# A hybrid attention layer on one core: loads of the opening in other pieces and places, columns of the modulation moved between projections, and gated linear attention's decay scans spread over its levels

## The chip, the cores and the metric

The kernel runs on one core of a Trainium2 chip. The metric is device time in microseconds for one execution. TensorE (PE) multiplies, VectorE (DVE) and ScalarE (ACT) do the elementwise work, GpSimd (POOL) does a little of it and issues some loads, and SyncE (SP) issues nearly all loads.

## The reference

One layer of a diffusion transformer in fp32, with 256 latent tokens and 256 context tokens of width 2048:

```python
h  = rms_norm(x,   g_mix) * (1 + scale_x) + shift_x      # scale, shift from silu(c) @ w_mod
hc = rms_norm(ctx, g_mix) * (1 + scale_c) + shift_c
qa, ka, va, qb, kb, vb, rb, lrf, lrb, gate_a, gate_b = split(h @ w_in)   # and of hc
o_attn = windowed_attention(qa, ka, va, cka, cva, sink)  # 16 heads, 4 for keys, sink logit
gf = log_sigmoid(lrf @ w_gate_f + b_gate_f) / 16         # 4 heads of 256; gb for the other way
o_gla = gla(qb, kb, vb, gf, gb)                          # both directions, from context's end states
x = x + gate * merge(o_attn, o_gla, rb, gate_a, gate_b)  # w_attn_o, w_gla_o, w_out
x = x + gate2 * conv_ffn(modulate(x, ...))               # w_up, conv of width 3, SwiGLU, w_down
```

Gated linear attention (GLA) weighs the product of a query and a key by the exponential of the decay summed between their two tokens.

## The kernel before, in words

**Weights.** A block of `w_in` of 256 rows by 512 columns is loaded as fp32 (`raw`, `wload`), split by ACT into a rounded part `whi` and by DVE into the rest `wlo` (`wsplit_raw`), and multiplied in three products: high by high, high by low of the tokens, low by high (`proj_nat`, `proj_T`). All loads of a queue go out in program order. The engines' orders are set when the kernel is built: mostly by a scheduler that follows the program, and in places by hand (`in_order`, `pin`).

**The opening.** 1 MB loads of `w_mod` (`mraw`) give the columns of scale and shift: `mod_both` makes one step per load. A step's products (`pm`) go into one bank; behind the last step DVE transposes it (`mtr`), and `end` turns it back to columns on PE (`pcol`). Groups of 2, 2, 4, 4 and 4 tiles of 128 channels follow each other: for each, the scale's columns, then the shift's, then `affine_scale` and `affine_shift` (tokens `xr` into `h00hi`, `h00lo` for the latent ones, `h10hi`, `h10lo` for context), then the group's part of four projections: GLA's queries (QB), keys (KB) and values (VB) of its first half. In the first group, a0, a1, ea are the two steps and the end of the scale, b0, b1, eb those of the shift. Sums of squares for the norm are products `pr`. `idle(n)` puts n products without use (`warm`) onto PE. In later groups the steps of the next group's columns stand in the middle of the projections: `mid` takes the next number from a list,

```python
steps = iter([1, 2, 1, 2, 2, 0])
```

and does so many steps of `bg_steps`.

**GLA.** Behind the groups, four projections go on, each beside one GLA head (`with_gla`). The head is a generator, `gla_A`: it goes on by one `yield` at a fraction of the projection's ticks, 0.91. First come the gates (`pz`, with a chain on ACT and DVE), then eight levels: at level `lv` DVE and ACT make queries and keys that carry the decay inside segments of 2^lv tokens (`q2`, `k2`, segment sums `segs`), and one level later PE multiplies them (`pa`), from which DVE takes a mask's part (`at`). At the end come the context's keys: two running sums of the decay (`kf`, `kg`, scans on DVE), exponentials on ACT, multiplications by the keys, and PE's last `pa`. Between ticks a second list of steps works at the rate `bg_rate`: columns of later modulations on DVE (`mod_latent`, the row at L365) with loads of their own.

**POOL's queue.** The attention sink is loaded by POOL's first DMA, rows of 16 numbers to each partition. Other small loads (`cw`, `lm`, the gates' weights) stand behind `gate`, an instruction on POOL that waits for the last columns.

Of the kernel before, what the change touches and what calls it, by code (L numbers as in the profile page):

```python
# [31 lines left out]
def layer_kernel(ctx, tc, A, out):  # L32
# [90 lines left out]
    def load_tokens(s):  # L123
        for i in range(4):
            k = slice((i % 2) * 4, (i % 2) * 4 + 4)
            load(xr[2 * s + i // 2][:, k, :], A["ctxT" if s else "xT"][i // 2, :, k, :])

# [61 lines left out]
    def wload(src):  # L189
        n = src.shape[0] // P  # L190
        raw = wr.tile([P, 2, 512], F32, name="raw", tag="raw")
        load(raw[:, 0:n, :], src.rearrange("(c p) d -> p c d", p=P))
        return raw

# [110 lines left out]


    def mod_both(part, t0, n, dst, put=None):

        a = []
        w = n * P  # L310
        nk = 16 // n

        def step(k0):
            if k0 == 0:
                a.append(bank(f"pm{part}_{t0}", (P, w), side=True))
            raw = M("mraw", [P, nk, w])
            load(raw, A["w_mod01"][part, t0 + k0 // nk].rearrange("p (c d) -> p c d", c=nk))
            for k in range(nk):
                kt = k0 + k
                q = 32 * (kt % 4)  # L320
                mm_b(a[0][q:q + 32, :], cS[:, kt, :], raw[:, k, :], start=(kt < 4), stop=(kt >= 12))
            if k0 == KT - nk:
                tr = W2("fb", "mtr", [P, n, 4, 32])
                V.transpose(tr.rearrange("p a b c -> p (a b c)"), a[0])
# [71 lines left out]
    def rms_scale(ss, n, shape):  # L396
# [15 lines left out]
    mods = [[mod_both(part, t0, n, dst, put) for part, dst in ((1, scale1), (0, shift1))]  # L412
            for (t0, n), put in zip(groups, [None, None] + 3 * [lambda fn: defer(0, fn)])]

# [4 lines left out]
    def square_sums(s):  # L419
# [3 lines left out]
        for i in range(4):  # L423
            x_ = xr[2 * s + i // 2][:, (i % 2) * 4:(i % 2) * 4 + 4, :]
            q = wr.tile([P, 4, T], F32, name="sq", tag="raw")
            if s + i:
                S.activation(q, x_, AF.Square)
# [55 lines left out]
    def affine_scale(s, t0, n):  # L483
        sc = scale1[:, s, t0:t0 + n]
        V.scalar_tensor_tensor(sc, sc, 1.0, gm1[:, t0:t0 + n], op0=ALU.add, op1=ALU.mult)
        for kt in range(t0, t0 + n):
            xk = xr[2 * s + kt // 8][:, kt % 8, :]
            V.scalar_tensor_tensor(xk, xk, scale1[:, s, kt:kt + 1], rrow1[s], op0=ALU.mult, op1=ALU.mult)

# [39 lines left out]
    factor_row(pr)  # L529
    a0()  # L530
    a1()
    idle(4)
    ea()
    b0()
    affine_scale(0, *groups[0])
    b1()
    raws = [wload(w_in[0:2 * P, c:c + 512]) for c in (QB, QB + 512)]
    idle(4)
# [5 lines left out]
    early.extend(raws)  # L544
    raws = [wload(w_in[0:2 * P, c:c + 512]) for c in (KB, VB)]
    load_tokens(1)
    i, j = affine_shift(0, *groups[0])
    hold.append(i)
    hold_hi.extend([None, j])
    proj_T(w_in, QB, kts, [h_all(0)], add_to(lambda i: qb0[i], True))  # L550
    proj_T(w_in, QB + 512, kts, [h_all(0)], add_to(lambda i: qb0[2 + i], True))
    wk, wv = wsplit_raw(raws[0]), wsplit_raw(raws[1])
# [43 lines left out]
    for gi, (t0, n) in enumerate(groups):  # L596
# [8 lines left out]
        if gi + 1 < len(groups):  # L605
# [3 lines left out]
            if gi == 1:  # L609
                bg_rate[:] = [0.0, 0.0]  # L610
                steps = iter([1, 2, 1, 2, 2, 0])

                def mid():
                    pin[0] = last[0]
                    for _ in range(next(steps)):
                        bg_steps.pop(0)()
                    pin[0] = None
        if t0 == 8:
            more_h(1)
        for s in range(2):  # L620
            if gi > 1:
                affine_scale(s, t0, n)
                affine_shift(s, t0, n)
            if s == 0:
# [80 lines left out]
    def gla_A(h, kb, qb, res):  # L705
# [7 lines left out]
        for d in range(2):  # L713
            g_ = W2("fc", "gc", [P, 2, T])
            for dt in range(2):
# [10 lines left out]
                V.tensor_tensor((PF if d == 0 else SB)[:, dt, :], mn[:, 0:T], e[:, 0:T], op=ALU.add)  # L726
# [30 lines left out]
        for lv in range(8):  # L757
# [21 lines left out]
            V.tensor_tensor(pfR, pfR, pfL[:, :, m - 1:m].to_broadcast([P, n, m]), op=ALU.add)  # L779
            V.tensor_tensor(sbL, sbL, sbR[:, :, 0:1].to_broadcast([P, n, m]), op=ALU.add)  # L780
# [14 lines left out]
        kf = W2("fa", "kf", [P, 2, T])  # L795
        kg = W2("fa", "kg", [P, 2, T])
        tot = sm.tile([P, 2], F32, name="tot", tag="tot", bufs=2)
        one = ones[:, 0:1].to_broadcast([P, T])
        for dt in range(2):
            V.tensor_tensor_scan(kf[:, dt, :], one, gc[0][:, dt, :], 0.0, op0=ALU.mult, op1=ALU.add)  # L800
            V.memset(kg[:, dt, 0:1], 0.0)
            V.tensor_tensor_scan(kg[:, dt, 1:T], ones[:, 0:1].to_broadcast([P, T - 1]), gc[1][:, dt, 0:T - 1], 0.0,
                                 op0=ALU.mult, op1=ALU.add)
        V.tensor_scalar(tot, kf[:, :, T - 1], -1.0 / 16, None, op0=ALU.mult)
        for dt in range(2):
            S.activation(kf[:, dt, :], kf[:, dt, :], AF.Exp, scale=1.0 / 16, bias=tot[:, dt:dt + 1])
        S.activation(kg, kg, AF.Exp, scale=-1.0 / 16)
        V.tensor_tensor(kf, kf, kc, op=ALU.mult)
        V.tensor_tensor(kg, kg, kc, op=ALU.mult)
        yield  # L810
# [39 lines left out]
    bg_steps.extend(mod_latent(((3, shift2), (4, scale2), (2, gcol1))))  # L850
    bg_rate[:] = [0.3, 0.0]

# [39 lines left out]
    G.dma_start(norms[:, 1, :], A["k_norm"][0].partition_broadcast(P))  # L892
    sink = cst.tile([P, 16], F32, name="sink")
    G.dma_start(sink, A["attn_sink"][0].partition_broadcast(P))
    for i, r in enumerate((rq, rk)):
# [131 lines left out]

    bg_rate[0] = 0.52
    rg = rms_scale(ssg, 512, [P, 4, 2])
# [288 lines left out]
```

## Time and profile before

| | us |
|---|---|
| time, median of 3 runs | 1982.68 (1981.75 to 1982.88) |
| the profiled execution | 1981.3 |
| its span | 1979.5 |
| PE busy | 1955.1 |
| DVE busy | 1399.8 |
| ACT busy | 972.1 |
| POOL busy | 44.2 |

The stages in the span: 0 to 25 us tokens' norm and the first columns; 25 to 73 the first group's projections, context's norm and the next columns; 73 to 204 the other groups; 204 to 460 GLA's four heads beside projections; then attention, the output projections and the ConvFFN, up to 1979.5. Rows of the stages give the busy time of each engine, with the number of instructions, then the clock that PE was granted (1.00 is full), the share of the DMA engines and GB/s. Rows of waits give the engine and the tile that waited, for which engine and tile it waited, the total, the number and the longest. In rows of the timeline a bracket holds the idle time before and what ended it. Durations overlap where instructions are pipelined.

### The profile page before, as it was taken

The page shows a single profiled execution, that of the slowest core. Times are in us where ns is not written, and L with a number is a line of the kernel's source. Part 1 is how long each engine was busy: PE and PEld are TensorE (multiplying, and loading weights), DVE is VectorE, ACT ScalarE, POOL GpSimd, SP SyncE. Part 2 cuts the span into 40 slices and gives each one's busy share as a digit, 9 for nine tenths or more (in the row PEclk, how much of TensorE's full clock was granted, in tenths as well). Part 3 has the DMA queues.
Part 4 walks back from the last instruction along what each step waited for, and adds up shares of the span by engine and source line. Part 5 has one row for each costly group of instructions (what it writes and reads, how often), then busy time and mean ns, then how long its engine had stood idle before and what let it go on. Part 6 is the DMA issues. An engine that isn't in the chain of part 4 may idle for free.

```text
span 1979.5 us, 27075 instructions
## 1 busy us (share of the span) xinstructions
PE 1955.1 (99%) x10292; PEld 1636.0 (83%) x10292; DVE 1399.8 (71%) x2150; ACT 972.1 (49%) x1415; POOL 44.2 (2%) x60
## 2 busy tenths in 40 slices
PE   7999999999999999999999999999999999999999
PEld 5679988888887778888888888888888888888887
DVE  5756767876767988777766467989886555677754
ACT  4323555552345666444444445755555334555533
POOL 0010010012000000000000000000000000000000
PEclk9999999999999999999999999999999999999999
DMA  9966222336754456888888677688886566666563
GB/s 379 413 258 185 75 85 78 93 108 205 233 160 118 127 181 213 268 290 292 289 286 265 235 236 262 198 271 285 257 274 228 193 197 188 187 190 189 188 216 109
DMA packets 183666, 420.88 MB, mean 213 GB/s; under 512 B 12544, under 2 KB 12768, under 8 KB 178800
## 3 DMA queue, kind: packets, MB, share of 16 engines
q1 hardware_dynamic: 182000, 413.45, 63.9%
q0 software_dynamic: 1360, 5.54, 1.0%
q8 instruction: 80, 1.31, 0.3%
q14 instruction: 50, 0.41, 0.1%
q10 hardware_dynamic: 176, 0.17, 0.0%
HBM read 416.98 MB, written 2.13 MB: 212 GB/s over the span
## 4 chain that ended last, share of the span: by engine, by line
PE 68%; DVE 0%; ACT 0%; issue 0%; DVEq 0%
PE acc L83 52%; PE accs L83 12%; PE poa L95 1%; PE pS L95 1%; PE ptp L98 1%; PE pto L98 0%; PE ptx L98 0%; DVE wlo L208 0%; ACT s L986 0%; PE ptq L98 0%; DVE s L991 0%; DVE yd L1238 0%; DVE yd L1232 0%; DVE raw L365 0%; ACT whi L207 0%
## 5 line engine op out<-in xcount | busy, mean ns | idle before, releaser
L208 DVE TENSOR_TENSOR wlo<-raw,whi 128x1024 fp32r<-128x1024 f32 x568 | 694.1, 1223 | 439.9 <-ACT whi L207 396.4
L207 ACT ACTIVATE whi<-raw 128x1024 fp32r<-128x1024 f32 x568 | 601.5, 1060 | 765.9 <-PE acc L83 608.9
L83 PE MATMUL accs<-h,whi 128*128 128x512 f32 x704 | 176.3, 392 | 0.0
L83 PE MATMUL acc<-h,whi 128*128 128x512 f32 x640 | 160.4, 392 | 0.0
L83 PEld LDWEIGHTS accs<-h,whi 128*128 128x128 f32 x704 | 126.6, 189 | 22.7
L83 PE MATMUL acc<-whi,h01hi 128*128 128x512 f32 x352 | 139.9, 398 | 0.0
L83 PE MATMUL acc<-whi,h00hi 128*128 128x512 f32 x352 | 138.9, 395 | 0.0
L83 PE MATMUL acc<-whi,h00lo 128*128 128x512 f32 x352 | 138.1, 392 | 0.0
L83 PE MATMUL acc<-whi,h01lo 128*128 128x512 f32 x352 | 137.8, 392 | 0.0
L83 PE MATMUL acc<-whi,ah 128*128 128x512 f32 x352 | 137.0, 389 | 0.0
L83 PE MATMUL acc<-whi,al 128*128 128x512 f32 x352 | 137.0, 389 | 0.0
L83 PEld LDWEIGHTS acc<-h,whi 128*128 128x128 f32 x640 | 115.0, 189 | 20.6
L83 PEld LDWEIGHTS accs<-h,wlo 128*128 128x128 f32 x704 | 96.0, 190 | 6.9
L83 PE MATMUL acc<-wlo,h01hi 128*128 128x512 f32 x352 | 98.7, 396 | 0.0
L83 PE MATMUL accs<-h,wlo 128*128 128x256 f32 x704 | 98.2, 282 | 0.0
L83 PE MATMUL acc<-wlo,h00hi 128*128 128x512 f32 x352 | 97.8, 394 | 0.0
L83 PE MATMUL acc<-wlo,ah 128*128 128x512 f32 x352 | 94.3, 389 | 0.0
L83 PEld LDWEIGHTS acc<-h,wlo 128*128 128x128 f32 x640 | 87.4, 190 | 6.3
L83 PE MATMUL acc<-h,wlo 128*128 128x256 f32 x640 | 89.4, 282 | 0.0
L365 DVE CUSTOM_DVE_ANT_0 raw<-raw,csrow,pack 128x1024 f32<-128x1024 f32 x64 | 81.4, 1281 | 0.0
L83 PEld LDWEIGHTS acc<-whi,ah 128*128 128x128 f32 x352 | 66.1, 188 | 13.7
L83 PEld LDWEIGHTS acc<-whi,al 128*128 128x128 f32 x352 | 66.1, 188 | 13.7
(377 smaller groups left out, 3558.1 us busy)
## 6 DMA issues: line engine op xcount, KB each, us to landing
raw<-in_w_in SPq DMA_DIRECT2D x208, 512.0 KB, 4.2
raw<-in_w_up SPq DMA_DIRECT2D x176, 512.0 KB, 4.1
raw<-in_w_modT SPq DMA_DIRECT2D x128, 512.0 KB, 4.4
raw<-in_w_down SPq DMA_DIRECT2D x88, 512.0 KB, 3.6
mraw<-in_w_mod SPq DMA_DIRECT2D x32, 1024.0 KB, 12.1
raw<-in_w_attn_o SPq DMA_DIRECT2D x32, 512.0 KB, 5.0
raw<-in_w_gla_o SPq DMA_DIRECT2D x32, 512.0 KB, 5.1
raw<-in_w_out SPq DMA_DIRECT2D x32, 512.0 KB, 4.7
```

The lines of the kernel that those rows point to most:

```text
L83: r = pe_seq(PE.matmul(*a, **k))
L95: return pe_seq(after(PE.matmul(*a, **k)))
L98: return pe_seq(after(PE.transpose(*a)))
L207: j = S.activation(hi[:, 0:n, :], raw[:, 0:n, :], AF.Copy).ins
L208: i = V.tensor_tensor(lo[:, 0:n, :], raw[:, 0:n, :], hi[:, 0:n, :].bitcast(F32), op=ALU.subtract).ins
L365: i0 = V.tensor_tensor_reduce(out=raws[i], in0=raws[i], in1=row[0], scale=1.0, scalar=d if h else bmod[:, b0:b0 + 1], op0=ALU.mult, op1=AL ...
```

## The change

Loads of the opening:

```diff
-        for i in range(4):
-            k = slice((i % 2) * 4, (i % 2) * 4 + 4)
-            load(xr[2 * s + i // 2][:, k, :], A["ctxT" if s else "xT"][i // 2, :, k, :])
+        for i in range(2):
+            load(xr[2 * s + i], A["ctxT" if s else "xT"][i])
...
+    def first_w(i):
+        raw = wr.tile([P, 2, 512], F32, name="raw", tag="raw")
+        load(raw.rearrange("p k d -> p (k d)"), A["w_first"][i])
+        return raw
...
+            if t0 < 4 and part == 0 and k0:
+                load(raw[:, 0:nk // 2, :], src[:, 0:nk // 2, :])
+                load(raw[:, nk // 2:nk, :], src[:, nk // 2:nk, :])
+            else:
+                load(raw, src)
...
+    data["w_first"] = np.stack([data["w_in"][0, 0:2 * P, c:c + 512].reshape(2, P, 512).transpose(1, 0, 2).reshape(P, 1024)
+                                for c in (QB, QB + 512, KB, VB)])
```

Tokens are loaded in two pieces of 1 MB, and a partition's row is 8 KB instead of 4; the first four blocks of `w_in` lie in memory so that a row is 4 KB instead of 2; the second load of the shift of the first two groups is cut in two.

Order of the opening: `idle(6)` is put in twice, squares of the context are ordered behind the evacuation of the first queries, the second group's columns and the context's keys change places:

```diff
     a0()
+    idle(6)
     a1()
     idle(4)
     ea()
     b0()
     affine_scale(0, *groups[0])
+    idle(6)
     b1()
...
-    a0()
     add_up(0, 2)
     factor_row(pr)
+    a0()
     a1()
     affine_scale(1, *groups[0])
     affine_shift(1, *groups[0])
+    b0()
     ea()
-    b0()
-    b1()
-    for s in range(2):
-        affine_scale(s, *groups[1])
+    affine_scale(0, *groups[1])
     early.extend([wk, wv])
-    proj_T(w_in, KB, kts, [h_all(1)], lambda i, b: S.activation(half(i, T), pair_of(b), AF.Copy), mid=eb)
+    proj_T(w_in, KB, kts, [h_all(1)], lambda i, b: S.activation(half(i, T), pair_of(b), AF.Copy), mid=b1)
+    eb()
...
+    affine_scale(1, *groups[1])
...
-                steps = iter([1, 2, 1, 2, 2, 0])
+                steps = iter([1, 2, 1, 4, 0, 0])
+                also = iter([next_columns] * 3 + [scale_2, next_columns, lambda: affine_shift(0, *groups[2])])
```

`next_columns` does a pending `end` of the third group; `scale_2` does that and the third group's `affine_scale`.

On PE, around the context's keys (`acc<-h10hi`), the second group's columns (`pm_2`, `pcol_2`) stood like this before:

```order
L95 MATMUL pm_2_389<-mraw,cS 32x256 x8
L448 MATMUL pr<-sq,ones 128x256 x2
L95 MATMUL pm_2_389<-mraw,cS 32x256 x8
L95 MATMUL pcol_2_429<-mtr,pack 32x16
L95 MATMUL pm_2_436<-mraw,cS 32x256 x16
L83 MATMUL acc<-h10hi,whi 128x256
```

and now stand like this (with the rest of the keys' products between the last `acc` that is shown first and the next `pm`):

```order
L462 MATMUL pr<-sq,ones 128x256 x2
L95 MATMUL pm_2_408<-mraw,cS 32x256 x16
L95 MATMUL pm_2_438<-mraw,cS 32x256 x8
L95 MATMUL pcol_2_449<-mtr,pack 32x16
L83 MATMUL acc<-h10hi,whi 128x256
...
L95 MATMUL pm_2_438<-mraw,cS 32x256 x8
L83 MATMUL acc<-h10hi,wlo 128x256 x8
L95 MATMUL pcol_2_500<-mtr,pack 32x16
```

The norm's sums came to the front, and the last eight column products went from before the keys into their middle.

On PE, in the second group's keys (`acc<-h10lo,whi` is the last product with the high part), the third group's shift (`pm_4`) before:

```order
L83 MATMUL acc<-h10lo,whi 128x256
L95 MATMUL pm_4_673<-mraw,cS 32x512 x8
L83 MATMUL acc<-h00hi,wlo 128x256
...
L95 MATMUL pm_4_673<-mraw,cS 32x512 x8
L95 MATMUL pcol_4_724<-mtr,pack 32x32
L83 MATMUL acc<-whi,h00hi 128x512
```

and now:

```order
L83 MATMUL acc<-h10lo,whi 128x256
L95 MATMUL pcol_4_676<-mtr,pack 32x32
L95 MATMUL pm_4_693<-mraw,cS 32x512 x16
L83 MATMUL acc<-h00hi,wlo 128x256
...
L95 MATMUL pcol_4_740<-mtr,pack 32x32
L83 MATMUL acc<-whi,h00hi 128x512
```

All 16 products of the shift stand in one place now, ahead of the 16 products with the low part, and the products with `whi` on the left that follow are the values.

The sink's load moves behind the gate, and in GLA the gates are made in four pieces instead of two, the scans and keys are made inside the levels, and the rates change:

```diff
+    sink = cst.tile([P, 16], F32, name="sink")
+    G.dma_start(sink, A["attn_sink"][0].partition_broadcast(P))
     lmask = cst.tile([P, 7, P], U8, name="lmask")
...
+                yield
             gc.append(g_)
-            yield
+
+        kf = W2("fb", "kf", [P, 2, T])
+        kg = W2("fb", "kg", [P, 2, T])
...
+        beside_levels = [[], [lambda i: scan_f(0, i)], [lambda i: scan_f(1, i)],
+                         [lambda i: scan_g(0, i), decay_f], [lambda i: scan_g(1, i)], [keys_f], [keys_g], []]
...
-            if lv == 1:
-                yield
             if lv:
                 products(lv - 1, *prev)
             prev = q2, k2
+            for fn in beside_levels[lv]:
+                fn(level)
             yield
...
-    bg_rate[:] = [0.3, 0.0]
+    bg_rate[:] = [0.0, 0.0]
...
-        beside[:] = [gla_A(h, kb, qbt, res), 0.91, 0.0]
+        beside[:] = [gla_A(h, kb, qbt, res), 0.97, 0.0]
...
-    bg_rate[0] = 0.52
+    bg_rate[0] = 0.62
```

`scan_f` and `scan_g` are the scans for one half of the channels, `decay_f` their total and the exponentials, `keys_f` and `keys_g` the multiplications (in `keys_g` behind its exponential), each ordered on DVE behind the last segment sum of its level. During GLA no modulation steps run any more; they run in the output projections at the higher rate.

On DVE, in the third level of the second head, before (`q_2902` and `k_2906` are the level's queries and keys):

```order
L751 COPY_PREDICATED at<-lmask,pa 128x256
L777 TENSOR_TENSOR segs<-segs 128x64x4
L768 TENSOR_TENSOR q_2902<-q_2902,qb 128x512
L775 TENSOR_TENSOR k_2906<-k_2906,kb_109 128x512
L778 TENSOR_TENSOR segs<-segs 128x64x4
L779 TENSOR_TENSOR segs<-segs 128x64x4
```

and now:

```order
L814 COPY_PREDICATED at<-lmask,pa 128x256
L770 SCALAR_TENSOR_TENSOR kf<-ones,gc 128x256
L840 TENSOR_TENSOR segs<-segs 128x64x4
L831 TENSOR_TENSOR q_2932<-q_2932,qb 128x512
L838 TENSOR_TENSOR k_2936<-k_2936,kb_107 128x512
L841 TENSOR_TENSOR segs<-segs 128x64x4
```

A scan (`kf<-ones,gc`) stands between two levels, ahead of the segment sums and the queries.

More of the change, by code (lines that the diff above doesn't have):

```diff
@@ L304, in layer_kernel @@
     ALL = list(range(KT))
+    folded = []
     def mod_both(part, t0, n, dst, put=None):
@@ L316, in step @@
             raw = M("mraw", [P, nk, w])
-            load(raw, A["w_mod01"][part, t0 + k0 // nk].rearrange("p (c d) -> p c d", c=nk))
+            src = A["w_mod01"][part, t0 + k0 // nk].rearrange("p (c d) -> p c d", c=nk)
+            if t0 < 4 and part == 0 and k0:
[3 more added lines that the diff above has]
+                load(raw, src)
             for k in range(nk):
@@ L323, in step @@
                 tr = W2("fb", "mtr", [P, n, 4, 32])
-                V.transpose(tr.rearrange("p a b c -> p (a b c)"), a[0])
+                folded[:] = [V.transpose(tr.rearrange("p a b c -> p (a b c)"), a[0]).ins]
                 a.append(tr)
@@ L412, in layer_kernel @@
     mods = [[mod_both(part, t0, n, dst, put) for part, dst in ((1, scale1), (0, shift1))]
-            for (t0, n), put in zip(groups, [None, None] + 3 * [lambda fn: defer(0, fn)])]
+            for (t0, n), put in zip(groups, [None, None] + [lambda fn: pend.append(fn)] + 2 * [lambda fn: defer(0, fn)])]
+    pend = []
     rrow1 = []
@@ L426, in square_sums @@
             if s + i:
-                S.activation(q, x_, AF.Square)
+                j = S.activation(q, x_, AF.Square).ins
+                if s and i in (0, 2):
+                    in_order(evicted[i + 1], j)
             else:
@@ L487, in affine_scale @@
             xk = xr[2 * s + kt // 8][:, kt % 8, :]
-            V.scalar_tensor_tensor(xk, xk, scale1[:, s, kt:kt + 1], rrow1[s], op0=ALU.mult, op1=ALU.mult)
+            i = V.scalar_tensor_tensor(xk, xk, scale1[:, s, kt:kt + 1], rrow1[s], op0=ALU.mult, op1=ALU.mult).ins
+            if s == 1 and kt < 2:
+                in_order(folded[0], i)
     def affine_shift(s, t0, n):
@@ L535, in layer_kernel @@
     affine_scale(0, *groups[0])
+    idle(6)
     b1()
-    raws = [wload(w_in[0:2 * P, c:c + 512]) for c in (QB, QB + 512)]
+    raws = [first_w(i) for i in range(2)]
     idle(4)
@@ L544, in layer_kernel @@
     early.extend(raws)
-    raws = [wload(w_in[0:2 * P, c:c + 512]) for c in (KB, VB)]
+    raws = [first_w(i) for i in range(2, 4)]
     load_tokens(1)
@@ L549, in layer_kernel @@
     hold_hi.extend([None, j])
-    proj_T(w_in, QB, kts, [h_all(0)], add_to(lambda i: qb0[i], True))
-    proj_T(w_in, QB + 512, kts, [h_all(0)], add_to(lambda i: qb0[2 + i], True))
+    evicted = []
+    for j in range(2):
+        proj_T(w_in, QB + j * 512, kts, [h_all(0)],
+               lambda i, b, j=j: evicted.append(S.activation(qb0[2 * j + i], b, AF.Copy).ins))
     wk, wv = wsplit_raw(raws[0]), wsplit_raw(raws[1])
@@ L610, in layer_kernel, with next_columns, scale_2 @@
                 bg_rate[:] = [0.0, 0.0]
-                steps = iter([1, 2, 1, 2, 2, 0])
+                steps = iter([1, 2, 1, 4, 0, 0])
+                def next_columns():
+                    if pend:
+                        pend.pop(0)()
+                def scale_2():
+                    next_columns()
+                    for s in range(2):
+                        affine_scale(s, *groups[2])
+                also = iter([next_columns] * 3 + [scale_2, next_columns, lambda: affine_shift(0, *groups[2])])
                 def mid():
                     pin[0] = last[0]
+                    next(also)()
                     for _ in range(next(steps)):
@@ L620, in layer_kernel @@
         for s in range(2):
-            if gi > 1:
+            if gi > 2:
                 affine_scale(s, t0, n)
+            if gi > 2 or (gi == 2 and s):
                 affine_shift(s, t0, n)
@@ L727, in gla_A, with scan_f, scan_g, decay_f @@
                 G.tensor_tensor(g_[:, dt, :], mn[:, T:2 * T], e[:, T:2 * T], op=ALU.add)
+                yield
             gc.append(g_)
-            yield
+        kf = W2("fb", "kf", [P, 2, T])
+        kg = W2("fb", "kg", [P, 2, T])
+        def scan_f(dt, level):
+            in_order(level, V.tensor_tensor_scan(kf[:, dt, :], ones[:, 0:1].to_broadcast([P, T]), gc[0][:, dt, :],
+                                                 0.0, op0=ALU.mult, op1=ALU.add).ins)
+        def scan_g(dt, level):
+            V.memset(kg[:, dt, 0:1], 0.0)
+            in_order(level, V.tensor_tensor_scan(kg[:, dt, 1:T], ones[:, 0:1].to_broadcast([P, T - 1]),
+                                                 gc[1][:, dt, 0:T - 1], 0.0, op0=ALU.mult, op1=ALU.add).ins)
+        def decay_f(level):
+            tot = sm.tile([P, 2], F32, name="tot", tag="tot", bufs=2)
+            in_order(level, V.tensor_scalar(tot, kf[:, :, T - 1], -1.0 / 16, None, op0=ALU.mult).ins)
+            for dt in range(2):
+                S.activation(kf[:, dt, :], kf[:, dt, :], AF.Exp, scale=1.0 / 16, bias=tot[:, dt:dt + 1])
+        def keys_f(level):
+            in_order(level, V.tensor_tensor(kf, kf, kc, op=ALU.mult).ins)
+        def keys_g(level):
+            S.activation(kg, kg, AF.Exp, scale=-1.0 / 16)
+            in_order(level, V.tensor_tensor(kg, kg, kc, op=ALU.mult).ins)
+        beside_levels = [[], [lambda i: scan_f(0, i)], [lambda i: scan_f(1, i)],
+                         [lambda i: scan_g(0, i), decay_f], [lambda i: scan_g(1, i)], [keys_f], [keys_g], []]
         at = sm.tile([P, 2, P], F32, name="at", tag="at", bufs=1)
@@ L779, in gla_A @@
             V.tensor_tensor(pfR, pfR, pfL[:, :, m - 1:m].to_broadcast([P, n, m]), op=ALU.add)
-            V.tensor_tensor(sbL, sbL, sbR[:, :, 0:1].to_broadcast([P, n, m]), op=ALU.add)
-            if lv == 1:
-                yield
+            level = V.tensor_tensor(sbL, sbL, sbR[:, :, 0:1].to_broadcast([P, n, m]), op=ALU.add).ins
             if lv:
@@ L794, in gla_A @@
             V.tensor_tensor(dst, dst, q_, op=ALU.mult)
[L795 to L809, printed above, removed]
         yield
@@ L892, in layer_kernel @@
     G.dma_start(norms[:, 1, :], A["k_norm"][0].partition_broadcast(P))
-    sink = cst.tile([P, 16], F32, name="sink")
-    G.dma_start(sink, A["attn_sink"][0].partition_broadcast(P))
     for i, r in enumerate((rq, rk)):
```

## The prediction

> **What bounds the kernel now.** I read the page's first and fourth parts, then the stages, then PE's waits inside the stages that the change touches, and last the timeline around those waits.
>
> ```profile
> span 1979.5 us, 27075 instructions
> PE 1955.1 (99%) x10292; PEld 1636.0 (83%) x10292; DVE 1399.8 (71%) x2150; ACT 972.1 (49%) x1415; POOL 44.2 (2%) x60
> PE 68%; DVE 0%; ACT 0%; issue 0%; DVEq 0%
> ```
>
> PE is the bound: it is busy for 99% of the span, and the chain that ended last lies on it. The change removes no product, so it can gain only what PE stands still or runs slowly. Per stage (microseconds, busy time of PE, PEld, DVE, ACT, POOL, then granted clock, DMA share, GB/s):
>
> ```profile
> 0.00:25.00 25.00, 16.43 (x114) 10.60 (x114) 9.74 (x29) 8.56 (x12) 1.39 (x6) 0.93 0.94 348
> 25.00:44.00 19.00, 17.33 (x154) 13.60 (x154) 13.39 (x24) 12.42 (x19) 0.00 (x0) 1.00 1.02 410
> 44.00:73.00 29.00, 26.83 (x200) 18.87 (x200) 20.90 (x49) 7.93 (x14) 0.00 (x0) 1.00 1.02 416
> 73.00:160.00 87.00, 86.33 (x638) 67.08 (x639) 54.87 (x108) 25.13 (x34) 6.27 (x12) 1.00 0.84 308
> 204.00:460.00 256.00, 250.36 (x1452) 215.42 (x1445) 192.20 (x361) 145.15 (x291) 27.17 (x27) 1.00 0.31 93
> ```
>
> PE is idle for 8.6, 1.7, 2.2, 0.7 and 5.6 us in these rows. Two places are open. Up to 73 us the DMA share is at its full 1.02, so there the loads are the second bound; from 204 to 460 (the four GLA heads beside the projections) DMA is at 0.31 and something else holds PE. PE's waits, first for 0 to 160 us, then for 200 to 460 us (total, times, longest):
>
> ```profile
> PE pm L95 <- DMA mraw<-in_w_mod: 3.0, 3, 1.4
> PE pcol L95 <- DVE mtr L324: 2.6, 4, 0.8
> PE acc L83 <- ACT h10hi L495: 0.7, 1, 0.7
> PE acc L83 <- ACT h00hi L495: 0.4, 1, 0.4
> ```
> ```profile
> PE pa L95 <- DVE q L768: 3.1, 4, 1.1
> PE pa L95 <- DVE kf L808: 2.5, 3, 1.0
> ```
>
> In GLA, 3.1 + 2.5 = 5.6 us, all of PE's idle time there: one wait per head for the first level's queries, and one for the final keys.
>
> **The opening.** The first term is the loads. Throughput between 3 and 11 us (40 slices of 0.2 us), and the share of POOL's queue:
>
> ```profile
> GB/s 365 356 336 404 390 423 348 469 489 348 369 440 177 18 20 20 41 82 205 205 246 451 389 348 389 430 369 369 389 430 328 471 389 492 410 451 410 451 410 420
> q0 software_dynamic: 36, 0.01, 16.6%
> ```
>
> From 5.4 to 7.2 us throughput falls as low as 18 GB/s while 0.01 MB of POOL's small packets (mainly the attention sink) use 16.6% of 16 engines for 8 us: 1.33 us of all engines. Moved behind the gate, the sink lands in the 73 to 160 stage, where DMA is at 0.84, and its first reader comes in attention, far behind: I cost it there at nothing. If that cover failed, it would cost the same 1.33 us.
>
> The second term is bigger rows for tokens and for the first four weight blocks. The nearest rows are the 44 to 73 stage above (416 GB/s, mostly 1 MB loads) and this one, which holds 512 KB loads and 1 MB loads:
>
> ```profile
> 20.00:40.00 20.00, 18.77 (x138) 14.62 (x142) 11.46 (x20) 12.84 (x18) 0.00 (x0) 0.91 1.03 410
> ```
>
> The tokens and blocks are 6.3 MB: 15.3 us at 410 and 15.1 at 416, a gain of 0.2 us; the mixed row hides some, so I take 0.3, from 0 to 0.6. All transfers behind them then land 1.33 + 0.3 = 1.65 us earlier. The two shift loads that are cut into 512 KB halves cost nothing by the same two rows (2.1 MB: 5.1 against 5.0 us), and let PE use one half while the other lands. The Trainium skill, "DMA: Bandwidth & Descriptors", section "Measured (HBM→SBUF, 128 partitions, SWDGE, issued from GpSimd)", speaks against that: batch to at least 1 MiB for 75% of peak or more. An estimate by it, halves at 75% of 416 GB/s, is 6.7 us, or 1.7 us lost; the 410 of the row that holds many 512 KB loads speaks against so large a loss.
>
> The third term is the clock. Two windows and PE's rows around them (start, duration):
>
> ```profile
> 16.71:20.12 3.41, 1.52 (x21) 0.55 (x18) 2.01 (x10) 0.00 (x0) 0.00 (x0) 1.00 0.98 407
> 20.12:23.54 3.42, 3.27 (x23) 1.63 (x24) 0.48 (x2) 1.06 (x1) 0.00 (x0) 0.50 1.05 390
> ```
> ```profile
> 15.28 1.07 PE L95 MATMUL pm<-mraw,cS 128*32 128x256 f32 x16 [1.01 <-DMA mraw<-in_w_mod]
> 17.78 1.07 PE L95 MATMUL pm<-mraw,cS 128*32 128x256 f32 x16 [0.62 <-DMA mraw<-in_w_mod]
> 20.27 1.93 PE L95 MATMUL pm<-mraw,cS 128*32 128x256 f32 x16 [1.43 <-DMA mraw<-in_w_mod]
> 24.96 0.39 PE L83 MATMUL acc<-h00hi,whi 128*128 128x256 f32 x1 [0.42 <-ACT h00hi L495]
> ```
>
> PE was busy for 1.52 of 3.41 us (45%), and for the next 3.42 us the granted clock was 0.50: the same 16 products took 1.93 us, not 1.07. The two inserted sets of six idle products fill those gaps. The half clock cost at most half of 3.42, 1.7 us; of that 0.9 is in these 16 products and the rest in warming and columns behind them, so I take 1.35. The Trainium skill, "TensorE: Matmul & The Clock Gate", section "HAM oscillation — how this bites in real kernels", asks only that PE not idle for more than some 3.4 us; by it the filling gains nothing and the sum would be 1.35 us less. The trace differs: the longest gap before the drop is 1.43 us. So the first product comes at 24.96 - 1.65 - 1.35 = 22.0.
>
> Behind it, the context's keys and values:
>
> ```profile
> 41.46 0.20 PE L95 MATMUL pcol<-mtr,pack 128*32 128x16 f32 x1 [0.57 <-DVE mtr L324]
> 44.15 0.38 PE L83 MATMUL acc<-h10hi,whi 128*128 128x256 f32 x1 [0.71 <-ACT h10hi L495]
> 62.26 0.25 PE L95 MATMUL pcol<-mtr,pack 128*32 128x32 f32 x2 [0.84 <-DVE mtr L324]
> 66.45 1.92 PE L95 MATMUL pm<-mraw,cS 128*32 128x512 f32 x16
> 73.16 0.25 PE L95 MATMUL pcol<-mtr,pack 128*32 128x32 f32 x2 [0.84 <-DVE mtr L324]
> ```
>
> Before, all four loads of the second group's columns stand ahead of the keys at 44.15, and DVE's transposes hold PE: 0.57 + 0.71 + 0.84 + 0.84 = 3.0 us. After, the last of these four loads stands in the middle of the keys, and each transpose has eight products or more over it; if that cover fails, the same 3.0 us return. Without another limit, the latent values of the second group, which begin behind the last of these rows at 73.4, would begin about 3.0 + 3.0 = 6.0 earlier. But another wait comes due: KB's middle now takes all four loads of the third group's shift in one go. Its last one (issue, then time to landing):
>
> ```profile
> L104 SPq DMA_DIRECT2D mraw<-in_w_mod x1: 328/328/328, 58.5 to 58.5; - x1
> DMA to landing us min/median/max: 9.4/9.4/9.4
> ```
>
> It lands at 67.9, and 1.65 earlier at 66.3. Behind it stand its four column products (by the row at 66.45, 16 in 1.92: 0.5 us), 16 products of 256 columns (26.83 us by 200 instructions in the 44 to 73 row is 0.13 each: 2.1 us, a little much, as that row holds larger ones too) and a row of columns turned back: 0.5 + 2.1 + 0.25 = 2.9, and with some 0.1 until the first of them can start the values begin at 69.3. The opening gains 73.4 - 69.3 = **4.1 us**; its bounds are 2.5 (loads 1.0 earlier, and the steps in between only half hidden) and 6.0. From 73 to 160 PE has 0.7 us of idle time in all, so nothing there can take it back.
>
> **GLA.** The rows that fix the levels: first and last level of the third head, on DVE and on PE.
>
> ```profile
> 352.57 0.68 DVE L768 TENSOR_TENSOR q<-q,qb 128x512 f32<-128x512 f32 x1
> 353.17 0.41 DVE L780 TENSOR_TENSOR segs<-segs 128x256 f32<-128x256 f32 x1
> 378.21 0.68 DVE L775 TENSOR_TENSOR k<-k,kb 128x512 f32<-128x512 f32 x1
> ```
> ```profile
> 353.30 1.16 PE L95 MATMUL pa<-q,kb 128*128 128x128 f32 x8 [0.35 <-DVE q L768]
> 380.87 1.05 PE L95 MATMUL pa<-q,k 128*128 128x128 f32 x8
> ```
> ```profile
> L365 DVE CUSTOM_DVE_ANT_0 raw<-raw,csrow,pack 128x1024 f32<-128x1024 f32 x12 | 15.3, 1281 | 0.0
> L800 DVE TENSOR_TENSOR_SCAN kf<-ones,gc 128x256 f32<-128x256 f32 x8 | 5.5, 683 | 3.4 <-PE pa L95 3.4
> L802 DVE TENSOR_TENSOR_SCAN kg<-ones,gc 128x255 f32<-128x255 f32 x8 | 5.5, 683 | 0.0
> L808 DVE TENSOR_TENSOR kf<-kf,kb 128x512 f32<-128x512 f32 x4 | 2.8, 688 | 0.4 <-ACT kf L806 0.4
> L726 DVE TENSOR_TENSOR segs<-gm,ge 128x256 f32<-128x256 f32 x16 | 10.5, 659 | 7.3 <-ACT ge L725 7.2
> ```
>
> Both waits go: the gates come in four pieces spread over more of the projection, and scans and keys have long been done when the final products come. What is late next is DVE in the levels. There it needs from 353.25 to 378.89, 25.6 us, with one modulation step (1.28) in it that the change removes. Added are four scans (2.73), two multiplications (1.37) and a small one: at most 4.2, and as an instruction of 0.68 us is followed after 0.60 (352.57 to 353.17), 3.8. So 25.6 - 1.3 + 3.8 = 28.2 us, against PE's 27.57, which the new order, with some two products of 512 columns fewer between those two levels, shortens to about 27.1. That leaves a new wait of 1.1 us a head in three heads and, in the first, whose projection is longer between levels, 0.5: 3.8 us. Against 5.6 us that is -1.8, and with a little less refilling of PE behind each stop **-2.0 us**. Bounds: all waits gone and no new ones, -7 (5.6 and 0.35 for each of four restarts); or new ones of 1.9 a head more than removed, +2.
>
> The 12 modulation steps of 1.28 us go to later stages, where DVE is free for a quarter or more of the time: nothing, and at worst 0.3 us for their loads.
>
> **Sum.** 1981.3 us is the profiled execution, 1979.5 its span; it lies 1.4 under the median 1982.7. -4.1 - 2.0 = -6.1: 1975.2 in that execution's terms, 1976.6 for the median.
>
> **Rivals.**
>
> *The levels hide everything.* DVE overlaps PE where I let it wait: then GLA gains 5.6 to 7 and the sum is -9.7 to -11.1, 1971.6 to 1973. For it: PE's groups wait for single levels, not for the whole chain. Against: DVE's idle time between levels is nearly nil. 0.17.
>
> *The half clock comes again.* In KB's middle PE now waits twice, for loads that land 2.5 us apart, about 0.8 and 1.5 us between 61 and 66 us. If it is busy for less than about half of a 3.4 us window there, the next runs at 0.50: 1.7 us lost, 1978.3. Against: the wait of 1.01 us at 15.28 was followed by a clock of 1.00. By the same section of the Trainium skill as above this rival would not occur, as no gap is near 3.4 us. 0.11.
>
> *The opening stays where the loads put it.* If the 1.33 us of POOL's packets only filled time that the queue recovers, landings stay, and keys wait for them: the opening gains 4.1 - 1.65 = 2.4 at most, 0 at worst; with GLA 1978.3 to 1980.7. For it: the DMA share of 1.02 up to 73 us. 0.15.
>
> *Round trips in the levels (slower).* A scan, its exponential on ACT and the multiplication now stand in DVE's order between level steps; each waits for ACT as the gate's row does (7.2 / 16 = 0.45 us). Six per head make 2.7: DVE's levels take 30.9 against 27.1, 3.8 us in three heads and 3.1 in the first, 14.5 against 5.6 removed: +8.9 - 4.1 = +4.8, 1987.5. It decides for slower from 29.5 us of DVE's levels on (27.1 plus a quarter of 5.6 + 4.1). For it: levels have hardly any idle time. Against: the change spreads the pieces one level apart, so ACT has a whole level for each. 0.12.
>
> **Numbers.** My forecast has 0.45, with a range of its own of 1973.5 to 1979.5. A measurement of this kernel can tell about 0.2% (4 us) from no change, so faster is under 1978.7 and slower above 1986.6. Faster: 0.42 of the forecast, 0.17 of the first rival, 0.07 of the second, 0.04 of the third: 0.70. Slower: 0.09 of the last: 0.09. The rest is 0.21. The range goes from 1970.0, just below the first rival, to 1982.5, which leaves out the last rival and a little at either end.
>
> **What would show it.** Right: the first product at about 22.0, no clock of 0.50 before it, landings of the third group's shift at 66.3, values of the second group at about 69; in GLA no wait for kf, and small waits of pa for q or k inside the levels. Wrong: the sink's dip staying in the first 11 us; a clock below 1 near 65; levels of more than 29.5 us; waits on modulated weights behind 460 us.

## The result, and the profile after

The median went from 1982.68 us to 1974.24 (1973.72 to 1975.00, 5 runs): ratio 0.9961, interval 0.9949 to 0.9973. Forecast were 1976.6 and a range of 1970.0 to 1982.5. The profiled execution took 1973.7 us with a span of 1972.0, 7.5 under the span before; runs of before that were taken beside the experiments have medians of 1981.4 to 1981.6, so 7.2 us is the better size of the effect. The profiled execution of after is the shortest of its five (spans of 1972.0 to 1973.2 us). Stages of after (microseconds, busy time of PE, PEld, DVE, ACT, POOL, clock, DMA share, GB/s):

```profile
0.00:25.00 25.00, 17.21 (x134) 11.86 (x135) 11.31 (x31) 10.09 (x14) 0.82 (x5) 1.00 0.93 371
25.00:44.00 19.00, 17.82 (x163) 14.43 (x161) 14.72 (x31) 11.18 (x18) 0.00 (x0) 1.00 1.02 409
44.00:73.00 29.00, 27.79 (x204) 19.58 (x201) 20.29 (x46) 10.03 (x17) 0.00 (x0) 1.00 1.02 419
204.00:460.00 256.00, 252.60 (x1426) 219.25 (x1426) 183.63 (x348) 144.63 (x290) 28.71 (x35) 1.00 0.27 81
```

PE's idle time is down in all four: from 8.6, 1.7, 2.2 and 5.6 us to 7.8, 1.2, 1.2 and 3.4. That is 4.5 us of the 7.5. PE's busy time fell too, from 1955.1 to 1952.8 us, though it has twelve products more: before, some ran slower (the clock of the first row was 0.93) or started further apart. PE's waits of after, for the opening (the first fence, without the smaller ones) and for GLA:

```profile
PE pm L95 <- DMA mraw<-in_w_mod: 1.2, 1, 1.2
PE acc L83 <- ACT h10hi L511: 0.7, 1, 0.7
```
```profile
PE pa L95 <- DVE k L838: 2.6, 6, 0.5
PE pa L95 <- DVE q L831: 0.7, 1, 0.7
```

Of the 5.6 us on the first level's q and on kf nothing is left; in their place PE waits 3.3 us for single levels. The steps of the opening, on PE's timeline of after:

```profile
19.94 1.07 PE L95 MATMUL pm<-mraw,cS 128*32 128x256 f32 x16
23.30 0.39 PE L83 MATMUL acc<-h00hi,whi 128*128 128x256 f32 x1 [0.46 <-ACT h00hi L511]
40.43 0.38 PE L83 MATMUL acc<-h10hi,whi 128*128 128x256 f32 x1 [0.67 <-ACT h10hi L511]
66.52 1.07 PE L95 MATMUL pm<-mraw,cS 128*32 128x512 f32 x8 [1.22 <-DMA mraw<-in_w_mod]
69.79 0.50 PE L83 MATMUL acc<-whi,h00hi 128*128 128x512 f32 x1
```

The first product comes 1.7 us earlier, the context's keys 3.7, and the second group's values, at 69.79, about 3.6. GLA's heads begin with the gates; the second and the third head before and after:

```profile
274.59 0.62 PE L95 MATMUL pz<-wgl 128*128 128x512 f32 x2
339.08 0.62 PE L95 MATMUL pz<-wgl 128*128 128x512 f32 x2
```
```profile
270.24 0.39 PE L95 MATMUL pz<-wgl 128*128 128x512 f32 x1
333.14 0.39 PE L95 MATMUL pz<-wgl 128*128 128x512 f32 x1
```

From head to head it is 62.9 us instead of 64.5.

### The profile page after: what moved, and what is told of

It reads as the page before. It is cut to its first block, busy times and chain, and to the rows that moved or that the text cites. A ratio compares the mean times of both kernels' runs of the same rounds, so it can differ in the third digit from the quotient of the medians.

```text
span 1972.0 us, 27091 instructions
## 1 busy us (share of the span) xinstructions
PE 1952.8 (99%) x10304; PEld 1635.6 (83%) x10304; DVE 1396.9 (71%) x2150; ACT 971.6 (49%) x1415; POOL 39.9 (2%) x60
## 3 DMA queue, kind: packets, MB, share of 16 engines
q8 instruction: 81, 1.33, 0.3%
## 4 chain that ended last, share of the span: by engine, by line
PE 94%; DVE 3%; ACT 1%; DMA 1%; issue 1%; ACTq 0%; DVEq 0%
PE acc L83 72%; PE accs L83 12%; PE pa L95 2%; PE poa L95 1%; PE pS L95 1%; PE po L95 1%; PE pm L95 1%; DVE wlo L212 1%; PE ptp L98 1%; DMA mraw<-in_w_mod 1%; ACT whi L211 0%; DVE q L831 0%; PE pto L98 0%; DMA pack<-in_k_pack 0%; DVE k L838 0%
```

## The experiments

Times are medians. The kernel before has 1981.37 us beside the first four runs and the last four, 1981.58 beside the second four. After itself was not run again beside them, so its 1974.24 is compared with theirs only together with the spans of the profiled executions, and differences of well under 1 us are not read. As after's span of 1972.0 is the shortest of its five, differences by the spans lie up to some 0.5 us too high for a slower kernel and too low for a faster one.

**The two halves apart.** e1 is the opening's half with GLA as before, e2 GLA's half with the opening as before (`gla_A`, both rates, 0.97).

> Only the opening's half of the change (loads, sink behind the gate, idle products, moved columns); GLA, its rates and the modulation's rates as before. If the two halves simply add, GLA begins 3.6 us earlier as in the changed kernel and the time is 3.6 us under before (about 1979). If GLA's gain depends on the opening, the time is nearer to 1974 or nearer to 1983.

> Only GLA's half (four gate pieces, scans and keys in the levels, rates); the opening as before. If the halves add, GLA begins at 209.6 us as before and the time is 3.9 us under before (about 1978.8), with some 3.3 us of waits on the levels' q and k and none on kf. My forecast's price for this half was 2.0 us (about 1980.7).

e1 took 1977.64 us (-3.7; ratio 0.9980, 0.9972 to 0.9989), e2 1977.87 (-3.5; 0.9982, 0.9973 to 0.9991). Together -7.2, which is what the whole change does: the halves add. The forecast's opening of 4.1 was nearly right, its GLA of 2.0 too small by 1.5. GLA's own length, from the first `pz` to the last head's first output product (`po`), does not depend on the opening: it is 254.4 us in e1 as in before, and 250.6 us in e2 as in after.

**The sink.** e3:

```diff
-    sink = cst.tile([P, 16], F32, name="sink")                    # behind the gate
-    G.dma_start(sink, A["attn_sink"][0].partition_broadcast(P))
...
     G.dma_start(norms[:, 1, :], A["k_norm"][0].partition_broadcast(P))
+    sink = cst.tile([P, 16], F32, name="sink")
+    G.dma_start(sink, A["attn_sink"][0].partition_broadcast(P))
```

> The changed kernel with the sink's load back as POOL's first DMA. If the packets' share is the price, the third group's last shift load lands 1.33 us later (67.8 instead of 66.5 us) and the time is 1.3 us longer (about 1975.5). If the dip is only time that the queue gets back, landings and time stay within 0.3 us of the changed kernel.

1975.04 us with a span of 1973.4: 0.8 more than after, and 1.4 by the spans of the profiled executions. POOL's queue is back with its share between 3 and 11 us, and the third group's last shift load with the values behind it come 1.3 us later than in after:

```profile
q0 software_dynamic: 32, 0.01, 14.8%
```
```profile
67.83 1.06 PE L95 MATMUL pm<-mraw,cS 128*32 128x512 f32 x8 [1.42 <-DMA mraw<-in_w_mod]
71.11 0.50 PE L83 MATMUL acc<-whi,h00hi 128*128 128x512 f32 x1
```

So 0.01 MB in small packets does cost all loads behind it about what its share of the engines says, 1.3 us. In the profiled execution all of that reaches GLA (its first `pz` at 207.3 us, in after at 206.0); in the medians 0.8 us of it is left.

**The idle products.** e4 is after without them, f4 is before with them:

```diff
     a0()
-    idle(6)
     a1()
...
     affine_scale(0, *groups[0])
-    idle(6)
     b1()
```

> The changed kernel without the two sets of six idle products. If they hold the clock, a window of 3.4 us at 0.50 comes back before the first product, which comes 1 to 1.4 us later than 23.3 us; by the landing at 66.5 us the delay is hidden for the most part, since PE waits 1.2 us there: time 0 to 0.4 us longer (1974.2 to 1974.6). If a granted clock below 1 does not come back, nothing changes.

> The kernel before with the two sets of six idle products and nothing else of the change. If they hold the clock, no window before 25 us has a granted clock below 1, the first product comes at 23.7 to 24.2 us instead of 25.0, and the time is 0 to 1 us shorter, as far as the loads behind allow. If PE's gaps for loads are what drops the clock, the window of 0.50 stays.

e4 took 1974.12 us, f4 1981.35 (1.0001, 0.9992 to 1.0010): nothing in either. But for two reasons. The two windows of e4, then its first product:

```profile
16.71:20.12 3.41, 2.71 (x43) 1.39 (x39) 2.91 (x12) 0.00 (x0) 0.00 (x0) 1.00 0.99 392
20.12:23.54 3.42, 2.83 (x22) 2.04 (x19) 2.44 (x10) 2.69 (x4) 0.00 (x0) 1.00 1.05 424
```
```profile
22.47 0.38 PE L83 MATMUL acc<-h00hi,whi 128*128 128x256 f32 x1 [0.46 <-ACT h00hi L511]
```

With the other loads PE is busy for 2.71 of 3.41 us without any filling, and the clock stays at 1.00; the first product even comes 0.8 earlier than in after, so there the idle products hold it up; PE then waits longer at the landing near 67 us (1.42 us instead of 1.22). In f4 the same window has 2.35 us of work, and the clock stays up too:

```profile
16.71:20.12 3.41, 2.35 (x27) 1.21 (x25) 2.04 (x10) 0.00 (x0) 0.00 (x0) 1.00 0.99 410
20.12:23.54 3.42, 2.90 (x30) 1.83 (x30) 1.22 (x6) 1.51 (x3) 0.00 (x0) 1.00 1.05 390
```
```profile
23.65 0.38 PE L83 MATMUL acc<-h00hi,whi 128*128 128x256 f32 x1 [0.46 <-ACT h00hi L495]
32.03 0.39 PE L83 MATMUL acc<-h00hi,whi 128*128 128x256 f32 x1 [1.81 <-ACT qb L503]
```

The first product comes 1.3 us earlier than before, as much as the forecast took for the clock; but at 32.03 PE waits 1.81 us for the evacuation of the first queries, where it waited 0.4 in before. The 1.3 us are given back there.

**The wait at 66.5 us.** e7 puts the last shift step of the third group behind the keys:

```diff
-                steps = iter([1, 2, 1, 4, 0, 0])
+                steps = iter([1, 2, 1, 3, 1, 0])
-                also = iter([next_columns] * 3 + [scale_2, next_columns, lambda: affine_shift(0, *groups[2])])
+                also = iter([next_columns] * 3 + [scale_2, lambda: None, shift_2])   # shift_2: both of these
```

> The changed kernel with the third group's last shift step behind the second group's keys instead of in their middle, and its end in the values' middle. If the landing at 66.5 us sets the start of the values, PE's wait of 1.2 us there goes, the values begin 1.0 to 1.2 us earlier than 69.8 us, and the time is 0.8 to 1.2 us shorter (about 1973.2), unless the third group's first product then waits for its shift. If another thing sets it, the time stays.

1973.80 us with a span of 1972.0, not to be told from after. The values begin 1.5 us earlier, but the third group's first product only 0.9 (after's is at 76.45, without a wait), and its first three products are spread over 0.74 us (0.34 in after), as they wait for shifted tokens:

```profile
68.25 0.50 PE L83 MATMUL acc<-whi,h00hi 128*128 128x512 f32 x1
...
75.60 0.38 PE L83 MATMUL acc<-h00hi,whi 128*128 128x256 f32 x1 [0.19 <-ACT h00hi L511]
...
76.34 0.28 PE L83 MATMUL acc<-h00hi,whi 128*128 128x256 f32 x1
```

GLA's first `pz` stands at 206.1 us, in after at 206.0.

**The scans in the levels.** e6 keeps the rest of GLA's half, and makes scans, exponentials and keys behind the last level:

```diff
             prev = q2, k2
-            for fn in beside_levels[lv]:
-                fn(level)
             yield
...
+        for fns in beside_levels:
+            for fn in fns:
+                fn(level)
         yield
         yield
```

> The changed kernel with the scans, exponentials and multiplications of the final keys behind the last level again (four gate pieces, rates and the missing modulation steps stay). If the scans in the levels cause the remaining waits, those on q and k (3.3 us) go and the wait on kf comes back, 0.8 to 1.1 us a head in three or four heads: 2.5 to 4 us, so the time is 0 to 1 us longer (1974.2 to 1975.5), and moving the scans by itself was worth next to nothing. If it was the main gain, the time rises by 2.5 us or more.

1970.81 us (0.9944, 0.9931 to 0.9956): 3.4 us *faster* than after, and 2.9 by the spans (1969.1). PE's waits in GLA, and the next two heads' starts:

```profile
PE pa L95 <- DVE kf L785: 1.6, 1, 1.6
```
```profile
270.31 0.39 PE L95 MATMUL pz<-wgl 128*128 128x512 f32 x1
331.90 0.39 PE L95 MATMUL pz<-wgl 128*128 128x512 f32 x1
```

All waits on levels are gone, 61.6 us from head to head. So it is the scans and keys in the levels that make after's new waits, as the forecast's DVE sum had it (3.8 us), but their move is not what removed the old waits: behind the levels they are in time for three heads of four. (e6 is not the order of before in all: both scans of kf come first in it, and kf is multiplied ahead of kg.)

**The modulation steps.** e5 is after with them in GLA, f1 is e6 with them (`bg_rate` 0.3 in GLA, 0.52 later).

> The changed kernel with modulation steps in GLA again (rate 0.3, then 0.52), so 12 steps of 1.28 us stand in DVE's order there. If DVE bounds the levels, each step inside them comes on top of the waits: about 0.9 step a head, 1.2 us, so the waits on q and k grow from 3.3 to 6 to 9 us and the time by 3 to 5 us (1977 to 1979). If the steps fall where DVE has time, waits stay at 3.3 us and the time stays at 1974.2.

> The kernel with the scans behind the last level, and modulation steps in GLA again (rate 0.3, then 0.52). In before, one step of 1.28 us stands right ahead of the multiplication that makes kf, in the third head, where PE then waits 1.0 us for kf. If such steps made the waits on kf, they come back, 1 to 1.3 us in two or three heads, and the time is 2 to 4 us above 1970.8. If the new buffers of kf and kg (which no longer wait for PE's last level) removed the waits, the time stays within 0.6 us of 1970.8.

e5 took 1972.92 us, 1.3 *less* than after (0.9 by the spans), f1 1970.51, as e6. Both expectations of a loss fell. In e5 15 steps run between 200 and 460 us, in after 6, all of them behind 441 us:

```profile
L376 DVE CUSTOM_DVE_ANT_0 raw<-raw,csrow,pack 128x1024 f32<-128x1024 f32 x15 | 19.0, 1280 | 0.0
```

and e5's waits on q and k are 2.8 us, in 4 places instead of 7:

```profile
PE pa L95 <- DVE k L838: 2.0, 3, 1.1
PE pa L95 <- DVE q L831: 0.8, 1, 0.8
```

Of e5's gain 0.7 us lies in GLA (249.9 us from the first `pz` to that `po`, 250.6 in after), and 0.3 behind it (1515.1 us to the end, 1515.4 in after): moved out of GLA, the steps cost a little where they went. Why the levels wait less with the steps among them was not found. In f1 the steps stand in GLA too, but none right ahead of the multiplication that makes kf.

**The gates' pieces.** f2 is e6 with two products in a piece and the levels at the same ticks:

```diff
                 G.tensor_tensor(g_[:, dt, :], mn[:, T:2 * T], e[:, T:2 * T], op=ALU.add)
-                yield
             gc.append(g_)
+            yield
+            yield
```

> The kernel with the scans behind the last level, and the gates in two pieces of two products instead of four of one, with the levels at the same ticks. If the finer gates removed the waits on the first level's q (3.1 us in before), these come back, 0.4 to 1.1 us a head: time 2 to 4 us above 1970.8. If the later start of the levels removed them, the time stays at 1970.8.

1970.94 us, as e6, and no wait on q. The pieces are worth nothing by themselves; by the expectation's other branch it is the later start of the levels, which f2 keeps.

**The last wait on kf.** In e6's last head, on DVE, a modulation step of the next stage stands between the scans and kf's multiplication:

```profile
438.07 1.28 DVE L376 CUSTOM_DVE_ANT_0 raw<-raw,csrow,pack 128x1024 f32<-128x1024 f32 x1
...
439.27 1.22 DVE L212 TENSOR_TENSOR wlo<-raw,whi 128x1024 fp32r<-128x1024 f32 x1
440.41 0.94 DVE L785 TENSOR_TENSOR kf<-kf,kb 128x512 f32<-128x512 f32 x1
```

f3 orders it behind the keys:

```diff
             in_order(last_lo[0], i0)
+            if last_key[0] is not None:
+                in_order(last_key[0], i0)
```

> The kernel with the scans behind the last level, with the modulation steps that follow GLA ordered behind the last head's final keys on DVE. If the step of 1.28 us ahead of kf's multiplication causes the one wait on kf that is left (1.6 us in the last head), the wait falls to 0.3 us or less and the time to about 1969.5. If the chain of scans and exponentials is too long by itself, it stays at 1970.8.

1969.40 us (0.9938, 0.9924 to 0.9951), the fastest of all: 4.8 under after. What is left of PE's waits in GLA:

```profile
PE pa L95 <- DVE kg L793: 0.2, 1, 0.2
```

**Keys on POOL.** e8 multiplies the final keys on POOL:

```diff
-            in_order(level, V.tensor_tensor(kf, kf, kc, op=ALU.mult).ins)
+            G.tensor_tensor(kf, kf, kc, op=ALU.mult)
```

and kg in the same way.

> The changed kernel with the two multiplications of the final keys (0.68 us each on DVE, per head) on POOL, about 1.9 us each there. If DVE's time in the levels sets the waits, those on the late levels (0.3 to 0.7 us, behind keys_f) go, those on the fifth level (0.5 us, behind the scans) stay: waits 3.3 to about 1.7 us, time 1.5 us shorter (1972.7). If the round trips over ACT set them, nothing changes; if POOL's result is late, a wait on kf of up to 1 us a head comes (1975 to 1978).

1977.61 us, 3.4 *more* than after (3.9 by the spans). While POOL makes kf in e8, a multiplication on DVE takes 1.62 us, and ends 0.54 behind POOL's; the same one in after takes 0.69:

```profile
364.82 1.28 POOL L785 TENSOR_TENSOR kf<-kf,kb 128x512 f32<-128x512 f32 x1 [16.03 <-DVE kg L774]
```
```profile
365.02 1.62 DVE L838 TENSOR_TENSOR k<-k,kb 128x512 f32<-128x512 f32 x1 [0.29 <-ACT k L837]
```
```profile
362.47 0.69 DVE L838 TENSOR_TENSOR k<-k,kb 128x512 f32<-128x512 f32 x1 [0.29 <-ACT k L837]
```

The three of the 28 multiplications of L838 that begin while POOL makes kf take 1.57 to 1.62 us, all others at most 0.81. What DVE gives to POOL it loses again beside it, and just at the level that PE waits for: waits on k rise to 6.2 us in 8 places.

```profile
PE pa L95 <- DVE k L838: 6.2, 8, 1.4
```

## Why the prediction was right, and where its steps were not

*The number.* It is partly luck. The opening was priced 0.4 too high and GLA 1.5 too low, and some of the reasons that were given for GLA's gain fell, though the gain came.

*The loads.* Right in size at the end, wrong on the way. The third group's shift was forecast to land at 66.3 us; PE uses it from 66.52 on. The sink's 1.33 us are shown by e3. There the same load is used from 67.83 on, and in before it landed at 67.9: the bigger rows, priced at 0.3, show no more than 0.1 us (with whatever the cut of the two shift loads cost). The step "all transfers behind them then land 1.65 earlier" does not hold for the first shift: its last half was issued at 6.7 us and took 12.8 to land, so it landed at 19.5, some 0.7 before PE could use the whole load in before (20.27). PE begins with it at 19.94, behind six idle products. The first product, forecast for 22.0, came at 23.30, and without the idle products at 22.47 (e4): they had a price of 0.8 us there, which the forecast left out.

*The clock.* The mechanism and its 1.35 us are shown by f4, whose first product comes 1.3 us earlier than before's. In before, PE worked for 45% of a window and had a clock of 0.50 in the next; e2, with the same opening, did so again (1.41 of 3.41 us from 17.18 on, then 0.50). In f4 PE works for 2.00 of 3.41 us (59%) in one window and waits for 1.81 us in front of the row at 32.03, longer than the 1.43 us just ahead of before's fall, and the clock stays at 1.00:

```profile
28.22:31.63 3.41, 2.00 (x17) 1.79 (x15) 1.49 (x3) 3.19 (x4) 0.00 (x0) 1.00 1.04 423
31.63:35.05 3.42, 3.02 (x25) 3.02 (x26) 3.29 (x5) 3.42 (x6) 0.00 (x0) 1.00 1.01 422
```

So the length of the gap does not decide it here; the share of work would fit, with a limit between 45% and 59%. Wrong was that the idle products bring it about in this change (e4 keeps the clock without them) and that the time is kept. The Trainium skill, "TensorE: Matmul & The Clock Gate", section "HAM oscillation — how this bites in real kernels", would let the clock fall only after about 3.4 us without work; before's longest gap ahead of the fall was 1.43 us, so this trace does not agree.

*The landing at 66 us as the limit.* Right: values at 69.3 forecast, 69.8 measured, opening 4.1 forecast, 3.7 measured in e1. e7 shows that its removal alone brings nothing that can be told, since the third group's shifted tokens are late next. The second rival's drop of the clock did not come: the only wait there is 1.22 us.

*GLA.* The removed waits (5.6 us) and the new ones (3.8 forecast, 3.3 measured) are right, and so is DVE's sum: in the third head its levels take 28.0 us (end of the first row to end of the second), forecast 28.2.

```profile
346.82 0.69 DVE L831 TENSOR_TENSOR q<-q,qb 128x512 f32<-128x512 f32 x1
374.81 0.68 DVE L838 TENSOR_TENSOR k<-k,kb 128x512 f32<-128x512 f32 x1
```

The sum of -2.0 was 1.5 short (-3.5 in e2). e1 still has the old GLA, with these waits:

```profile
PE pa L95 <- DVE q L803: 3.2, 4, 1.1
PE pa L95 <- DVE kf L843: 2.5, 3, 1.0
```

The last head's first `po` ends the stretch in e1, in after and in e6; all three begin it at 206.0 or 206.1 us:

```profile
460.36 0.39 PE L95 MATMUL po<-v3h,ats 128*128 128x512 f32 x1
456.57 0.39 PE L95 MATMUL po<-v3h,ats 128*128 128x512 f32 x1
453.37 0.39 PE L95 MATMUL po<-v3h,ats 128*128 128x512 f32 x1
```

From e1 to after that is 3.8 us, and the waits give 2.4 of it. Of the 1.5 us that the sum was short, 0.5 are waits (3.3 us of new ones instead of 3.8). The term that was mis-sized is "a little less refilling of PE behind each stop", put at 0.2: 1.4 us stand in no wait of the profile, and 0.3 are lost again behind GLA, where the modulation steps went. A price per stop does not explain the 1.4 us, since after has seven stops as before has; what does stays open.

The price itself can be read where a stop is. Products of this kind last 0.39 us in a row, but the next one starts 0.22 to 0.23 us behind. The one behind 453.02 could have started at 453.25; it started 1.11 us later, and the row counts 0.94 from the end of the one ahead:

```profile
452.80 0.39 PE L83 MATMUL acc<-whi,h11hi 128*128 128x512 f32 x1
453.02 0.39 PE L83 MATMUL acc<-whi,h11lo 128*128 128x512 f32 x1
454.36 1.10 PE L95 MATMUL pa<-q,kf 128*128 128x256 f32 x4 [0.94 <-DVE kf L808]
```

So this stop cost 0.17 us beyond its wait, about half of the 0.35 that the forecast's bound took from no row. From after to e6 GLA is 3.3 us shorter: 1.7 us of waits, 1.0 for six stops fewer at that price, and 0.6 that is not explained.

*Why the old waits went.* Here the forecast's reasons fell, though its result held, and that is luck. "The gates come in four pieces" is worth nothing by itself (f2), "scans and keys have long been done" costs 3.4 us (e6), and the removed modulation steps, priced at 1.28 us a head, cost nothing where they stood (f1). What is left are the new spacing of the levels (gates with two yields more, so a later start; one yield fewer in the levels; rate 0.97), the new order of the scans and the keys' new buffers. Before, the scans waited 3.4 us for PE's last level, as the row of the prediction says; in e6 they wait for nothing:

```profile
L770 DVE TENSOR_TENSOR_SCAN kf<-ones,gc 128x256 f32<-128x256 f32 x8 | 5.1, 675 | 0.0
```

and in before a modulation step stands right ahead of kf's multiplication in the third head, and again in the fourth (at 452.32), so at two of the three waits on kf:

```profile
386.56 1.28 DVE L365 CUSTOM_DVE_ANT_0 raw<-raw,csrow,pack 128x1024 f32<-128x1024 f32 x1
...
387.76 0.69 DVE L808 TENSOR_TENSOR kf<-kf,kb 128x512 f32<-128x512 f32 x1
```

f3 shows for e6's last head that such a step makes the wait, and f1 does not speak against it, as none of its steps stands there. Spacing, order and buffers were not tried one by one, so which of them took away which wait of before stays open.

*The slower rival.* Its mechanism, DVE's own time in the levels, is real (e6), but as large as the forecast had it (28.0 us in the third head, not 30.9), not as round trips: in after no level waits more than 0.7 us. Its sign, more than 29.5 us, would have been only the point at which the change gains nothing.

## What to carry to other kernels

Before work is spread into a pipelined loop, add up what the loop's slowest engine already does in it: here DVE had, by the prediction's rows, about 2.7 us a head to spare in the levels and got 3.8, while the place behind them had cover in three heads of four. When a change is a bundle, undo each part alone: this one holds a part that costs 3.4 us (the scans in the levels) and two that do nothing (idle products, gate pieces), beside those that gain. A wait that is removed ahead of a load that lands later, or of an engine that is late next, comes back there (f4, e7): look for the next wait before counting the gain.

## What was not expected of the hardware

Small packets of 0.01 MB on POOL's queue held up all loads by 1.3 us (e3). A multiplication of 128x512 on POOL beside one on DVE made DVE's take 1.62 us instead of 0.69 (e8). PE's clock fell to 0.50 behind a window with 45% of work whose longest gap was 1.43 us, and did not behind one with 59% and a gap of 1.81 us (before, f4).
